# One hybrid attention, SSD and gating layer on one core: first B and C tiles made as a pair, modulation sums in two banks, a store and a norm moved

## Chip, core and metric

One core of a Trainium2 chip runs the whole layer in one launch. The metric is the device time in microseconds (us) of one launch. The kernel before was run three times; the profile is of a fourth execution, whose own time stands beside its span in the table below.

## What is computed

One layer of a diffusion backbone, for 128 context tokens and 512 latent tokens (640 columns together), width 2048. Cut to what matters here:

```python
m = silu(cvec) @ w_mod + b_mod;  shift, scale, gate = split(m, 3)
h = rms(x, g_pre) * (1 + scale) + shift
q, k, v, g_a, xbc, z, dt_raw, u, v_c, g_c, g_m = split(h @ w_in)
o_a = attention(q, k, v) * silu(g_a)
xbc = silu(dwconv(xbc));  x, B, C = split(xbc)      # B and C: 4 tiles of 128 channels each
o_b = rms(ssd(x, dt, B, C) * silu(z))
o_c = u * (w_s @ norm(v_c) + b_s) * silu(g_c)
merged = sigmoid(g_m) gates over o_a @ w_br_a, o_b @ w_br_b, o_c @ w_br_c
y = x + gate * rms(merged @ w_out, g_post)
```

All inputs are float32. The products are made from halves of 32-bit numbers: each operand is split into a high part (type fp32r) and the rest, and three matmuls (high by high, high by rest, rest by high) make one product.

## The kernel before

`h` has its 2048 channels on 16 blocks of 128 partitions, its 640 tokens along the free axis. A tile of 128 output channels is made on TensorE (PE) in one of two ways. `plain` (L208) runs over 16 channel blocks and two halves of 320 tokens: 16 x 2 x 3 = 96 matmuls of 320 columns. `pair` (L219) makes two tiles together by seven block products (in the manner of Strassen and Winograd), each over 8 blocks: 7 x 8 x 3 = 168 matmuls of 320 columns, where two plain tiles take 192. Its weights are combined on GpSimd (POOL, L190 to L198) and split into halves on ScalarE (ACT, `whi`, L166) and VectorE (DVE, `wlo`, L167).

The stages around the change, in the order of the program:

- **First stage** (L340 to L370). For each of 16 channel blocks k: `wm_block` (L262) loads 2 MB of modulation weights in four pieces and sums them on PE into one PSUM bank `m` (sixteen matmuls, L271, which the trace holds as 32 records); DVE copies the bank to `mrow` (L274); two small matmuls with `sel` (L349) turn the row into columns; DVE makes the factors (`mc`, L352, L353) and applies them (`xn`, L357); ACT makes the high half `hh` (L360) and DVE the rest `hl` (L361). Then PE makes the first 512 channels of `v_c` for that block (L331 to L333: ten matmuls with `hh`, five with `hl`, 512 columns each) and the first tile of B (`u`, L368: six matmuls of 320 columns). `h` is also stored to `h_d` in HBM (L359), since `make_t` later reads it back for the operands of the seven products.
- **Rest of v_c** (L381 to L398), then gating norm and mixing, and `dt`.
- **Plain tiles**: the first tile of C (`plain(NT_C, ...)`, with `post_conv` for it and for B's first tile, L635 to L638), then three tiles each of u and g_c; `make_t` and `make_t3` run beside them.
- **Pairs**: five of u and g_c, then the list `rest`: pairs of x, B, C (`xbc`, whose `post_conv` is four DVE operations of 642 columns for each tile), pairs of merge gates (`post_gate`, tanh on ACT), pairs of `silu` tiles, pairs of k, v, q. From the job with number `n0 - 1` on, `Pre` prepares the SSD beside the pairs: 36 steps, one with each of 36 pairs, with its own loads on the queue of SyncE (SP), exponentials on ACT, products on DVE.
- **SSD, attention, branch projections, output**, and at the end, for the last quarter of the output channels, norm, gate and residual (L1296 to L1324).

What sets the order: the scheduler of the framework takes the program's text in order, but places instructions of each engine by its own plan, so that an instruction can stand before others that the text has ahead of it. `issue_after` ties an instruction behind another. Every engine then runs its list in order, and so does SP's list of DMAs.

Of the kernel before, what the change touches and what calls it, by code (L numbers as in the profile page):

```python
# [7 lines left out]
F32 = mybir.dt.float32  # L8
F32R = mybir.dt.float32r
AF = mybir.ActivationFunctionType  # L10
# [24 lines left out]
def hybrid_step(ctx: ExitStack, tc: tile.TileContext, a: dict, o: dict):  # L35
# [106 lines left out]
    wseq = [("plain", NT_C)] + [("plain", n + g) for g in range(NF) for n in (NT_U, NT_GC)]  # L142
    wseq += [("pair", NT_U + g, NT_GC + g) for g in range(NF, 8)]
    gates = [("pair", NT_GM + 16 * b + d, NT_GM + 16 * b + d + 1) for b in (2, 1, 0) for d in range(0, KD, 2)]
    xbc = [(NT_X + t, NT_X + t + 1) for t in range(0, 8, 2)] + [(NT_B + 1, NT_B + 2), (NT_B + 3, NT_C + 1), (NT_C + 2, NT_C + 3)]
# [3 lines left out]
    for x in xbc:  # L149
        rest += [("pair", *x), gates.pop(0)]  # L150
# [127 lines left out]
    bt0 = cvp.tile([P, T], F32, tag="bt0", name="bt0")  # L278
# [44 lines left out]
    u_ps = [ps_tile("u0"), ps_tile("u1")]  # L323
    mps = ps_tile("m")
    vw, uw = {}, {}
# [10 lines left out]
    for k in range(KD + 2):  # L336
        if k < KD:
            mrow[k] = wm_block(wmp, a["w_ms"][k], mps, 9)
            if k % 2 == 0:
                vw[k], vw[k + 1] = load_w(a["w_v0"][:, k:k + 2, :], eng=G)  # L340
            if k % 8 == 0:
                for i, p_ in enumerate(load_w(a["w_nt"][NT_B, :, k:k + 8, :], wmp, "u", 2, eng=G)):
                    uw[k + i] = p_
        if 1 <= k <= KD:

            i = k - 1
            sl_ps = u_ps[0][:, HALF + 4 * i:HALF + 4 * i + 4]
            for s in range(2):
                TE.matmul(sl_ps[:, 2 * s:2 * s + 2], mrow[i][:, s * P:(s + 1) * P], sel, start=(i < 2), stop=True, skip_group_check=True)  # L349
# [12 lines left out]
        if k >= 2:  # L362
            i = k - 2
            v_block(i, range(NCH))
            uh, ul = uw[i]
            for w, x, first, last in ((uh, h_hi, i == 0, False), (uh, h_lo, False, False), (ul, h_hi, False, i == KD - 1)):
                for s in range(2):
                    TE.matmul(u_ps[s][:, :HALF], w, x[i][:, s * HALF:(s + 1) * HALF], start=first, stop=last)  # L368
    st.close()
    with ExitStack() as ph:  # L370
# [4 lines left out]
        for s in range(2):  # L375
            S.copy(bt0[:, s * HALF:(s + 1) * HALF], u_ps[s][:, :HALF])
# [135 lines left out]
    def halves(t):  # L512
        return [t[:, H1], t[:, H2]]

# [267 lines left out]
    n0 = 2 * len(xbc)  # L782
# [485 lines left out]
    for n in range(4):  # L1268
# [32 lines left out]
        for t in range(NCH):  # L1301
# [8 lines left out]
            V.tensor_tensor(ya[t, n], v_ps[t], gb[:, min(t, 1), :], op=ALU.mult)  # L1310
            rs = yp.tile([P, 1], F32, name=f"rs{t}")
            V.reduce_sum(rs, ssy[t], axis=mybir.AxisListType.X)
            rsqrt(rs, rs, 0.0625 / D)
            fin.append(rs)
            for f in {0: (), NCH - 1: (t - 1, t)}.get(t, (t - 1,)):
                dst = o["y_prompt"] if f == 0 else o["y_sample"][(f - 1) * P:f * P]
                for m in range(4):
                    if m == 1 or f < 3 and m == 2:
                        S.activation(ya[f, m], ya[f, m], AF.Copy, scale=fin[f])
                        G.tensor_tensor(xr[f][m], ya[f, m], xr[f][m], op=ALU.add)  # L1320
                    else:
                        V.scalar_tensor_tensor(out=xr[f][m], in0=ya[f, m], scalar=fin[f], in1=xr[f][m],
                                               op0=ALU.mult, op1=ALU.add)
                    nc.sync.dma_start(out=dst[:, m * 512:(m + 1) * 512], in_=xr[f][m])  # L1324
# [89 lines left out]
```

## Time and profile before

| what | value |
|---|---|
| time of a run, median of 3 (lowest to highest) | 2525.13 us (2521.27 to 2529.65) |
| profiled execution, own time | 2523.14 us |
| its span on the core | 2521.3 us |
| PE busy, share of the span | 2430.2 us, 96% |
| DVE, ACT, POOL busy | 1714.3, 1086.2, 805.0 us (68, 43, 32%) |
| mean DMA rate over the span | 163 GB/s |

Busy shares are means over stages with different limits. The rows below go by stage: the view by windows gives the busy time of each engine in a stretch, and the timeline gives single instructions.

### The profile page before, as it was taken

What the parts mean: (1) busy time and instruction counts of PE and PEld (TensorE: products, weight loads), DVE (VectorE), ACT (ScalarE), POOL (GpSimd) and SP (SyncE); (2) the same over time, 40 slices, a digit from 0 to 9 for tenths busy, and PEclk for the clock granted to TensorE, in tenths of its full rate; (3) what the DMA queues carried; (4) which work ended last, traced back from release to release, by engine and by line L of the source; (5) the groups of instructions that cost most, each with busy time, mean ns of one, the idle gap of its engine ahead of it and who ended that gap; (6) DMA issues with size and microseconds to landing.
All of it is one profiled execution on the core that took longest, in us unless ns stands there. A gap on an engine that the chain in (4) does not pass through costs nothing. (4 is left out here: it accounts for less than half of the span.)

```text
span 2521.3 us, 43204 instructions
## 1 busy us (share of the span) xinstructions
PE 2430.2 (96%) x16615; PEld 2298.9 (91%) x16615; DVE 1714.3 (68%) x2769; ACT 1086.2 (43%) x2343; POOL 805.0 (32%) x372
## 2 busy tenths in 40 slices
PE   6989999999999999999999999999999999999998
PEld 4569999999999999999999999989998888998886
DVE  5344688887888778767777677777544555537974
ACT  4122233444444555555555554555323666322222
POOL 2100044444434344434343344334232233331002
PEclk9999999999999999999999999999999999999999
DMA  9943533333333344543444444434987554445545
GB/s 379 351 164 101 164 113 118 105 116 115 105 110 115 130 147 133 161 160 128 150 143 136 137 128 156 143 121 155 333 311 249 174 182 135 155 123 193 177 142 166
DMA packets 154073, 411.13 MB, mean 163 GB/s; under 512 B 16966, under 2 KB 29547, under 8 KB 153867
## 3 DMA queue, kind: packets, MB, share of 16 engines
q1 hardware_dynamic: 151562, 407.33, 48.4%
q8 instruction: 130, 2.13, 0.4%
q10 hardware_dynamic: 2304, 1.05, 0.1%
q14 instruction: 77, 0.62, 0.1%
HBM read 333.50 MB, written 74.81 MB: 162 GB/s over the span
## 5 line engine op out<-in xcount | busy, mean ns | idle before, releaser
L167 DVE TENSOR_TENSOR wlo<-wraw,whi 128x512 fp32r<-128x512 f32 x448 | 607.5, 1373 | 128.7 <-ACT whi L166 120.8
L166 ACT CAST whi<-wraw 128x512 fp32r<-128x512 f32 x448 | 275.1, 616 | 314.9 <-PE acca L235 148.3
L135 ACT CAST whi<-wraw 128x512 fp32r<-128x512 f32 (+1 forms) x238 | 140.1, 592 | 415.6 <-PE bk L820 138.9
L236 PE MATMUL acca<-hh,wlo 128*128 128x320 f32 x896 | 280.5, 313 | 15.3 <-DVE wlo L167 15.3
L166 ACT CAST whi<-s 128x512 fp32r<-128x512 f32 x336 | 203.0, 617 | 207.9 <-PE sm L235 85.1
L167 DVE TENSOR_TENSOR wlo<-s,whi 128x512 fp32r<-128x512 f32 x336 | 232.8, 693 | 73.8 <-ACT whi L166 69.8
L234 PE MATMUL acca<-hh,whi 128*128 128x320 f32 x896 | 278.4, 311 | 0.9 <-ACT whi L166 0.9
L235 PE MATMUL acca<-hl,whi 128*128 128x320 f32 x896 | 277.5, 310 | 0.0
L190 POOL TENSOR_TENSOR s<-wraw 128x1024 f32<-128x1024 f32 x56 | 147.2, 2628 | 368.6 <-DMA wraw<-in_w_nt 226.8
L136 DVE TENSOR_TENSOR wlo<-wraw,whi 128x512 fp32r<-128x512 f32 (+1 forms) x218 | 154.5, 712 | 148.7 <-ACT whi L135 148.1
L191 POOL TENSOR_TENSOR s<-s,wraw 128x1024 f32<-128x1024 f32 x56 | 150.5, 2688 | 258.2 <-DVE wlo L167 258.1
L198 POOL TENSOR_TENSOR s<-wraw,s 128x1024 f32<-128x1024 f32 x56 | 138.6, 2475 | 209.8 <-issue 190.3
L236 PEld LDWEIGHTS acca<-hh,wlo 128*128 128x128 f32 x896 | 168.8, 188 | 21.7 <-DVE wlo L167 21.6
L234 PEld LDWEIGHTS acca<-hh,whi 128*128 128x128 f32 x896 | 169.2, 189 | 1.2 <-ACT whi L166 1.1
L235 PEld LDWEIGHTS acca<-hl,whi 128*128 128x128 f32 x896 | 169.0, 189 | 0.0
L820 PE MATMUL bk<-oh,whi 128*128 128x320 f32 x512 | 164.2, 321 | 0.7 <-DVE c L250 0.7
L820 PE MATMUL bk<-oh,wlo 128*128 128x320 f32 x512 | 158.9, 310 | 0.0
L820 PE MATMUL bk<-ol,whi 128*128 128x320 f32 x512 | 158.8, 310 | 0.0
L236 PE MATMUL sm<-t4h,wlo 128*128 128x320 f32 x448 | 141.6, 316 | 13.3 <-DVE wlo L167 13.3
L192 POOL TENSOR_TENSOR wraw<-wraw 128x1024 f32<-128x1024 f32 x56 | 151.8, 2710 | 4.3
L234 PE MATMUL sm<-t4h,whi 128*128 128x320 f32 x448 | 139.7, 312 | 2.4 <-ACT whi L166 2.4
L235 PE MATMUL sm<-t4l,whi 128*128 128x320 f32 x448 | 139.4, 311 | 0.0
(403 smaller groups left out, 6953.7 us busy)
## 6 DMA issues: line engine op xcount, KB each, us to landing
wraw<-in_w_nt SPq DMA_DIRECT2D x240, 512.0 KB, 3.8
wm<-in_w_ms SPq DMA_DIRECT2D x64, 512.0 KB, 7.1
wraw<-in_w_br SPq DMA_DIRECT2D x48, 512.0 KB, 4.5
wm<-in_w_mg SPq DMA_DIRECT2D x32, 512.0 KB, 3.9
wraw<-in_w_out SPq DMA_DIRECT2D x31, 512.0 KB, 3.9
g_gate<-sg SPq DMA_DIRECT2D x48, 320.0 KB, 2.4
gt<-g_gate SPq DMA_DIRECT2D x48, 320.0 KB, 4.5
ac_d<-Y SPq DMA_DIRECT2D x32, 256.0 KB, 3.4
```

The source lines that it names most:

```text
L135: S.copy(hi[:, :n], rv)
L136: eng.tensor_tensor(lo[:, :n], rv, hi[:, :n].bitcast(F32), op=ALU.subtract)
L166: S.copy(hi, src[:, i:i + 512])
L167: V.tensor_sub(lo, src[:, i:i + 512], hi.bitcast(F32))
L190: G.tensor_tensor(s1, a21, a22, op=ALU.add)
L191: G.tensor_tensor(s2, s1, a11, op=ALU.subtract)
L192: G.tensor_tensor(a21, a11, a21, op=ALU.subtract)
L198: G.tensor_tensor(s2, a12, s2, op=ALU.subtract)
L234: TE.matmul(ps, wh, bh, start=(k == 0 and i not in (2, 3)), stop=False, skip_group_check=True)
L235: TE.matmul(ps, wh, bl, start=False, stop=False, skip_group_check=True)
L236: mm = TE.matmul(ps, wl, bh, start=False, stop=(k == n - 1), skip_group_check=True)
L820: newest[0] = TE.matmul(*args, **kw)
```

## The change

Four edits, in the order of the program:

1. B's first tile is no longer made in the first stage (`u_ps` was two banks, its 96 matmuls and its two weight loads go). One of the two banks becomes a second bank for the modulation sums: `wm_block` alternates between `mps[0]` and `mps[1]`.
2. The store of `h` to `h_d` leaves the first stage's text. In the text of the rest of v_c, for each k, DVE now adds `hh` and `hl` to a tile `hs` and SP stores that.
3. C's first plain tile goes. B and C are now four pairs, so that `xbc` has eight pairs and not seven; the order of `rest` changes with it, and `n0` is 15 and not 14.
4. At the end, each token block's root is started ahead of its product with the gate row, on DVE and POOL; one of ACT's and POOL's pieces of a block goes to DVE; and the outputs of the block before are tied behind both.

```diff
-    wseq = [("plain", NT_C)] + [("plain", n + g) for g in range(NF) for n in (NT_U, NT_GC)]
+    wseq = [("plain", n + g) for g in range(NF) for n in (NT_U, NT_GC)]
...
-    xbc = [(NT_X + t, NT_X + t + 1) for t in range(0, 8, 2)] + [(NT_B + 1, NT_B + 2), (NT_B + 3, NT_C + 1), (NT_C + 2, NT_C + 3)]
+    xbc = [(NT_X + t, NT_X + t + 1) for t in range(0, 8, 2)] + [(NT_B + t, NT_B + t + 1) for t in range(0, 8, 2)]
...
     for x in xbc:
-        rest += [("pair", *x), gates.pop(0)]
+        rest.append(("pair", *x))
+    if x[0] != NT_C + 2:
+        rest.append(gates.pop(0))
...
-    u_ps = [ps_tile("u0"), ps_tile("u1")]
-    mps = ps_tile("m")
+    u_ps = ps_tile("u0")
+    mps = [ps_tile("m"), ps_tile("u1")]
...
-            mrow[k] = wm_block(wmp, a["w_ms"][k], mps, 9)
+            mrow[k] = wm_block(wmp, a["w_ms"][k], mps[k % 2], 9)
...
-            if k % 8 == 0:
-                for i, p_ in enumerate(load_w(a["w_nt"][NT_B, :, k:k + 8, :], wmp, "u", 2, eng=G)):
...
-            nc.sync.dma_start(out=h_dram[:, i, :], in_=hf)
...
-            uh, ul = uw[i]
-            for w, x, first, last in ((uh, h_hi, i == 0, False), (uh, h_lo, False, False), (ul, h_hi, False, i == KD - 1)):
...
+                        if blk == 0:
+                            hs = gp.tile([P, T], F32, tag=("raw", "sg", "c2")[k % 3], name="hs")
+                            V.tensor_tensor(hs, h_hi[k].bitcast(F32), h_lo[k].bitcast(F32), op=ALU.add)
+                            nc.sync.dma_start(out=h_dram[:, k, :], in_=hs)
...
-    post_conv(8, halves(bt0))
-    ac = two_banks()
-    plain(NT_C, ac)
-    post_conv(12, [b[:, :HALF] for b in ac])
...
-    n0 = 2 * len(xbc)
+    n0 = 2 * len(xbc) - 1
...
-            V.tensor_tensor(ya[t, n], v_ps[t], gb[:, min(t, 1), :], op=ALU.mult)
             rs = yp.tile([P, 1], F32, name=f"rs{t}")
             V.reduce_sum(rs, ssy[t], axis=mybir.AxisListType.X)
-            rsqrt(rs, rs, 0.0625 / D)
+            V.tensor_scalar(rs, rs, 0.0625 / D, EPS, op0=ALU.mult, op1=ALU.add)
+            root = G.tensor_tensor(rs, rs, mhalf[:, :1], op=ALU.pow)
+            gated = V.tensor_tensor(ya[t, n], v_ps[t], gb[:, min(t, 1), :], op=ALU.mult)
...
+                with tc.issue_after(gated.ins), tc.issue_after(root.ins):
...
-                    if m == 1 or f < 3 and m == 2:
+                        if m == 1:
```

How instructions stand in the built programs, at three places.

**PE in the first stage**, late in it: from the end of one block's `v_` matmuls to the start of the next block's. L271 and L273 are the modulation sums, L349 and L346 the small matmuls with `sel`. Before:

```order
L333 MATMUL v_466<-whi,hl_1292 128x512
L368 MATMUL u_468<-hl_1292,whi 128x320
L368 MATMUL u_468<-hh_133,wlo 128x320
L271 MATMUL m<-wm,cs 32x256 x12
L349 MATMUL u_467<-sel,mrow 128x2 x2
L271 MATMUL m<-wm,cs 32x256 x4
L368 MATMUL u_467<-hh_133,whi 128x320
L368 MATMUL u_467<-hl_1292,whi 128x320
L368 MATMUL u_467<-hh_133,wlo 128x320
L271 MATMUL m<-wm,cs 32x256 x4
L331 MATMUL v_462<-whi,hh_134 128x512
```

and now:

```order
L334 MATMUL v_465<-whi,hl_1193 128x512
L273 MATMUL u_468<-wm,cs 32x256 x4
L273 MATMUL m<-wm,cs 32x256 x4
L346 MATMUL u_466<-sel,mrow 128x2 x2
L273 MATMUL m<-wm,cs 32x256 x8
L332 MATMUL v_461<-whi,hh_134 128x512
```

The matmuls of B's tile are gone on both sides of the small ones; between the small matmuls and the next block's first there now stand modulation sums alone. The sums go to `m` and `u_468` in turn.

**DVE in the first stage**, one block late in it, from `hl` of one block to `hl` of the next. Before:

```order
L361 TENSOR_TENSOR hl_1166<-xn_115,hh_131 128x640
L274 COPY mrow<-m 128x256
L352 TENSOR_TENSOR mc<-u_467,pc 128x4
L353 TENSOR_SCALAR mc<-mc,pc 128x2
L357 TENSOR_SCALAR xn_116<-xn_116,mc 128x128
L357 TENSOR_SCALAR xn_116<-xn_116,mc 128x512
```

and now:

```order
L357 TENSOR_TENSOR hl_1081<-xn_115,hh_131 128x640
L381 TENSOR_TENSOR hs<-hh_131,hl_1081 128x640
L276 COPY mrow<-u_468 128x256
L349 TENSOR_TENSOR mc<-u_466,pc 128x4
L350 TENSOR_SCALAR mc<-mc,pc 128x2
L354 TENSOR_SCALAR xn_116<-xn_116,mc 128x128
L354 TENSOR_SCALAR xn_116<-xn_116,mc 128x512
```

and SP's list there, in the first stage too (L270 are the loads of modulation weights):

```order
L270 DMA wm<-in_w_ms 128x1024 x3
L125 DMA wraw<-in_w_v 128x544
L382 DMA h_d<-hs 128x640
L270 DMA wm<-in_w_ms 128x1024 x5
L382 DMA h_d<-hs 128x640
```

The new sum `hs` (L381), which the text has in the rest of v_c, is placed by the scheduler in the first stage, right behind `hl` and ahead of the next copy of `mrow`; all sixteen of them stand ahead of DVE's copies that end the stage. Their stores stand among the loads of modulation weights, as the stores of `xn` did.

**SP beside the pairs.** A pair of merge gates ends in two stores to `g_gate`, an x, B or C tile in two to `cv_d`, a `silu` tile in one to `sl_a` or `sl_b`; `ac_d` and `acum_d` belong to `Pre`. Early in `rest`, before:

```order
L529 DMA cv_d<-cv 128x128
L510 DMA cv_d<-cv 128x512
L184 DMA wraw<-in_w_nt 128x1024 x2
L510 DMA g_gate<-sg 128x640 x2
L184 DMA wraw<-in_w_nt 128x1024 x5
L529 DMA cv_d<-cv 128x128
```

and now:

```order
L186 DMA wraw<-in_w_nt 128x1024 x3
L520 DMA cv_d<-cv 128x128
L504 DMA cv_d<-cv 128x512
L186 DMA wraw<-in_w_nt 128x1024
L520 DMA cv_d<-cv 128x128
L504 DMA cv_d<-cv 128x512
```

The eight pairs of x, B and C now follow each other with no gate pair between. Behind them come the eight `silu` pairs, of which seven now have no step of `Pre` (before, all eight had one); the k, v, q pairs have twelve steps as before, and 23 gate pairs have one, where 16 had. A gate pair with its step of `Pre` stands as it did:

```order
L504 DMA g_gate<-sg 128x640 x2
L759 DMA ac_d<-Y 128x512
L672 DMA ssq<-acum_d 128x640
L186 DMA wraw<-in_w_nt 128x1024 x4
L504 DMA g_gate<-sg 128x640 x2
```

## Rows read from the trace of the kernel before

**Rows 1.** The page: busy time (share of the span) and instructions of the engines.

```profile
PE 2430.2 (96%) x16615; PEld 2298.9 (91%) x16615; DVE 1714.3 (68%) x2769; ACT 1086.2 (43%) x2343; POOL 805.0 (32%) x372
```

**Rows 2.** Windows, first stage and pairs: PE, PEld, DVE, ACT, POOL; clock; DMA share, GB/s.

```profile
20.00:80.00 60.00, 50.05 (x386) 31.24 (x383) 28.02 (x84) 15.42 (x38) 16.30 (x14) 0.97 1.03 407
35.00:160.00 125.00, 114.01 (x831) 73.80 (x831) 41.94 (x98) 21.99 (x35) 20.49 (x16) 0.99 0.87 324
398.90:472.90 74.00, 74.00 (x507) 74.00 (x506) 65.33 (x70) 29.27 (x53) 37.52 (x17) 1.00 0.35 113
```

**Rows 3.** One PE block of the first stage (start, length, engine, line).

```profile
63.19 0.50 PE L331 MATMUL v<-whi,hh 128*128 128x512 f32 x1 [0.55 <-ACT hh L360]
...
65.62 0.31 PE L368 MATMUL u<-hh,whi 128*128 128x320 f32 x1
65.87 0.64 PE L271 MATMUL m<-wm,cs 128*32 128x256 f32 x8
...
66.44 1.43 PE L333 MATMUL v<-whi,hl 128*128 128x512 f32 x5
...
67.70 0.31 PE L368 MATMUL u<-hl,whi 128*128 128x320 f32 x1
...
68.66 0.61 PE L349 MATMUL u<-sel,mrow 128*128 128x2 f32 x4
...
71.67 0.50 PE L331 MATMUL v<-whi,hh 128*128 128x512 f32 x1 [0.62 <-ACT hh L360]
```

**Rows 4.** The same chain late in the stage, from `sel` to the next block.

```profile
126.77 0.61 PE L349 MATMUL u<-sel,mrow 128*128 128x2 f32 x4
...
129.49 0.50 PE L331 MATMUL v<-whi,hh 128*128 128x512 f32 x1 [0.34 <-ACT hh L360]
```

**Rows 5.** First matmuls of the first block, and the last block's first.

```profile
35.85 0.80 PE L331 MATMUL v<-whi,hh 128*128 128x512 f32 x1 [1.96 <-ACT hh L360]
...
36.88 0.63 PE L331 MATMUL v<-whi,hh 128*128 128x512 f32 x1
...
160.37 0.50 PE L331 MATMUL v<-whi,hh 128*128 128x512 f32 x1 [1.15 <-ACT hh L360]
```

**Rows 6.** Waits of PE in the first stage (35 to 160 us): total, times, longest.

```profile
PE v L331 <- ACT hh L360: 7.0, 10, 2.0
PE m L271 <- DVE mrow L274: 2.7, 5, 0.5
```

**Rows 7.** POOL's split of weights and DVE's `hl` there: shortest, median, longest (ns).

```profile
L136 POOL TENSOR_TENSOR wlo<-wraw,whi x16: 1267/1276/1355, 37.8 to 134.6; 128x512 fp32r<-128x512 f32 x16
L361 DVE TENSOR_TENSOR hl<-xn,hh x16: 815/825/1421, 35.8 to 160.4; 128x640 fp32r<-128x640 f32 x16
```

**Rows 8.** From the first stage to the rest of v_c.

```profile
164.89 0.49 DVE L613 TENSOR_TENSOR ssq<-tb,ta 128x320 f32<-128x320 f32 x1 [3.71 <-DMA ta<-h_d]
...
167.23 1.88 DVE L374 COPY vc<-v 128x512 f32<-128x512 f32 x3
...
169.25 0.56 PE L391 MATMUL acca<-whi,hh 128*128 128x272 f32 x1 [4.30 <-DVE vc L374]
```

**Rows 9.** Each pair's one copy L240, by stretch: times, first and last start (us).

```profile
L240 ACT COPY u<-acca x15: 403/418/424, 472.9 to 827.2; 128x320 f32<-128x320 f32 x15
L240 ACT COPY u<-acca x9: 416/418/422, 852.3 to 1055.1; 128x320 f32<-128x320 f32 x9
L240 ACT COPY u<-acca x13: 407/418/419, 1055.1 to 1364.9; 128x320 f32<-128x320 f32 x13
L240 ACT COPY u<-acca x16: 402/405/408, 1364.9 to 1765.6; 128x320 f32<-128x320 f32 x16
```

**Rows 10.** Waits of PE beside seven x, B, C and seven gate pairs (473 to 827 us).

```profile
PE acca L236 <- DVE wlo L167: 5.7, 7, 0.8
```

**Rows 11.** The end: DVE's last two entries in the timeline.

```profile
2514.86 1.42 DVE L1322 SCALAR_TENSOR_TENSOR wraw<-y,rs,wraw 128x512 f32<-128x512 f32 x2 [0.66 <-POOL rs L115]
2516.19 0.75 DVE L1322 SCALAR_TENSOR_TENSOR wraw<-bk,rs,wraw 128x512 f32<-128x512 f32 x1
```

More of the change, by code (lines that the diff above doesn't have):

```diff
@@ L277, in hybrid_step @@
     dt_raw = cvp.tile([P, NCH, 32], F32, name="dt_raw")
-    bt0 = cvp.tile([P, T], F32, tag="bt0", name="bt0")
     psx = ExitStack()
@@ L322, in hybrid_step @@
     v_ps = [ps_tile(f"v{t}") for t in range(NCH)]
-    u_ps = [ps_tile("u0"), ps_tile("u1")]
-    mps = ps_tile("m")
-    vw, uw = {}, {}
+    u_ps = ps_tile("u0")
+    mps = [ps_tile("m"), ps_tile("u1")]
+    vw = {}
     def v_block(k, ts):
@@ L337, in hybrid_step @@
         if k < KD:
-            mrow[k] = wm_block(wmp, a["w_ms"][k], mps, 9)
+            mrow[k] = wm_block(wmp, a["w_ms"][k], mps[k % 2], 9)
             if k % 2 == 0:
                 vw[k], vw[k + 1] = load_w(a["w_v0"][:, k:k + 2, :], eng=G)
-            if k % 8 == 0:
-                for i, p_ in enumerate(load_w(a["w_nt"][NT_B, :, k:k + 8, :], wmp, "u", 2, eng=G)):
-                    uw[k + i] = p_
         if 1 <= k <= KD:
             i = k - 1
-            sl_ps = u_ps[0][:, HALF + 4 * i:HALF + 4 * i + 4]
+            sl_ps = u_ps[:, 4 * i:4 * i + 4]
             for s in range(2):
-                TE.matmul(sl_ps[:, 2 * s:2 * s + 2], mrow[i][:, s * P:(s + 1) * P], sel, start=(i < 2), stop=True, skip_group_check=True)
+                TE.matmul(sl_ps[:, 2 * s:2 * s + 2], mrow[i][:, s * P:(s + 1) * P], sel, start=True, stop=True)
             mc = wmp.tile([P, 2, 2], F32, tag="mc", name="mc")
@@ L362, in hybrid_step @@
         if k >= 2:
-            i = k - 2
-            v_block(i, range(NCH))
-            uh, ul = uw[i]
-            for w, x, first, last in ((uh, h_hi, i == 0, False), (uh, h_lo, False, False), (ul, h_hi, False, i == KD - 1)):
-                for s in range(2):
-                    TE.matmul(u_ps[s][:, :HALF], w, x[i][:, s * HALF:(s + 1) * HALF], start=first, stop=last)
+            v_block(k - 2, range(NCH))
     st.close()
@@ L374, in hybrid_step @@
             (S.copy if t % 2 else V.tensor_copy)(vc[:, t, 0:512], v_ps[t])
-        for s in range(2):
-            S.copy(bt0[:, s * HALF:(s + 1) * HALF], u_ps[s][:, :HALF])
         psx.close()
@@ L510, in store @@
         stored[0] = nc.sync.dma_start(out=out, in_=in_)
-    def halves(t):
-        return [t[:, H1], t[:, H2]]
     def post_conv(t, x):
@@ L1309, in hybrid_step @@
                 continue
-            V.tensor_tensor(ya[t, n], v_ps[t], gb[:, min(t, 1), :], op=ALU.mult)
             rs = yp.tile([P, 1], F32, name=f"rs{t}")
             V.reduce_sum(rs, ssy[t], axis=mybir.AxisListType.X)
-            rsqrt(rs, rs, 0.0625 / D)
+            V.tensor_scalar(rs, rs, 0.0625 / D, EPS, op0=ALU.mult, op1=ALU.add)
+            root = G.tensor_tensor(rs, rs, mhalf[:, :1], op=ALU.pow)
             fin.append(rs)
+            gated = V.tensor_tensor(ya[t, n], v_ps[t], gb[:, min(t, 1), :], op=ALU.mult)
             for f in {0: (), NCH - 1: (t - 1, t)}.get(t, (t - 1,)):
                 dst = o["y_prompt"] if f == 0 else o["y_sample"][(f - 1) * P:f * P]
-                for m in range(4):
-                    if m == 1 or f < 3 and m == 2:
[L1319 to L1324, printed above, removed]
+                with tc.issue_after(gated.ins), tc.issue_after(root.ins):
+                    for m in range(4):
+                        if m == 1:
+                            S.activation(ya[f, m], ya[f, m], AF.Copy, scale=fin[f])
+                            G.tensor_tensor(xr[f][m], ya[f, m], xr[f][m], op=ALU.add)
+                        else:
+                            V.scalar_tensor_tensor(out=xr[f][m], in0=ya[f, m], scalar=fin[f], in1=xr[f][m],
+                                                   op0=ALU.mult, op1=ALU.add)
+                        nc.sync.dma_start(out=dst[:, m * 512:(m + 1) * 512], in_=xr[f][m])
 def _layout(i):
```

## The prediction

> **What bounds the kernel now.** I read the page first, then windows by stage, then the timeline inside the stages that the change touches, and last the waits. The page says PE: 2430 us of the span [rows 1]. But that is a mean over stages, and two of them matter here. Between pairs PE is never idle: in three pairs it is busy 74.00 of 74.00 us, and DVE has 65.33 us of work beside it, ACT and POOL much less [rows 2]. So there a matmul costs 74.0/507 = 0.146 us, a pair 74.0/3 = 24.67 us, and what delays DVE may come through to PE. In the first stage PE is busy 114.0 of 125 us [rows 2], and a block is a chain: `sel` on PE, `mc` and `xn` on DVE, `hh` on ACT, back to PE's `v` matmuls. That wait is short, 0.55 to 1.15 us [rows 3 to 5], 7.0 us in ten waits [rows 6], only because matmuls of B's tile and modulation sums lie beside the chain. The DMA rate of 407 GB/s is high early in the stage (20 to 80 us) but falls to 324 over its length at a share of 0.87 [rows 2], and no wait of PE on a load is among the large ones, so I take it that loads set only the stage's start. The sixteen blocks' first matmuls run from 35.85 to 160.37 us [rows 5]: 124.5/15 = 8.30 us a block.
>
> **First stage.** What leaves it: per block six matmuls of B's tile. What does not leave it, whatever the text says: the sum `hs` and the store of `h`; the order has all sixteen in the stage. So part 2 of the change does not move the store in the built program, and adds sixteen DVE operations. None costs PE directly; the question is whether removed PE work was on the chain or filled its gaps. I build a block from the chain. Ten `hh` matmuls take 65.62 − 63.19 = 2.43 us, five `hl` 67.70 − 66.44 = 1.26, a group of four sums (eight records) 66.44 − 65.87 = 0.57 [rows 3]. From `sel` to the next block's first matmul it takes 71.67 − 68.66 = 3.01 us in the block of rows 3 and 129.49 − 126.77 = 2.72 in that of [rows 4]. In both PE had work for most of this and then still waited for `hh`; so it is the chain's own length, and removing the tile's matmuls from within it gives nothing. I take 2.72, since little beside it is left that can delay it.
>
> In the new order `sel` stands behind the five `hl` matmuls in thirteen of fifteen blocks: 13 x (2.43 + 1.26 + 2.72) = 83.3 us. In two it stands ahead of them: 2 x (2.43 + 2.72) = 10.3. The sums that stand ahead of `sel` are on the path: 28 groups of 0.57 us are 16.0, and 1.3 for starting them, from the 0.25 us between neighbours of different kinds (65.62 to 65.87) [rows 3]. Copies of the bank just ahead of `sel` in four blocks cost 2.7/5 = 0.54 us each [rows 6], less what a second bank takes away; I take 0.4, so 1.6. The first block starts at a slower pace, 36.88 − 35.85 = 1.03 us for two matmuls [rows 5] against 0.49; for five of them some 1.3. And DVE is slowed at times beside POOL: `hl` takes 0.815 us at best, 1.421 at worst [rows 7]; three such cases on the chain are 1.8. Sum 83.3 + 10.3 + 17.3 + 1.6 + 1.3 + 1.8 = 115.6, against 124.5: **−8.9**. The two weight loads of B's tile are 1.05 MB, of which half lies ahead of the first block: 0.52 MB at 407 GB/s is **−1.3**. Bounds: if the chain never shows, PE's sum for a block is 2.43 + 1.26 + 4 x 0.57 + some 0.5 = 6.5, so 15 x 1.8 = −27; if the pace stays 8.3 us, −1.3 alone.
>
> At the stage's end DVE now waits 3.71 us for `h_d` in an operation of `make_t`'s chain, and only behind it makes the copies `vc` that free PE, which stood 4.30 us [rows 8]. In the new order the copies stand ahead. The last `hs`, of the length of an `hl` (0.825 [rows 7]), stands ahead of them too, and by then DVE has nothing else to do. PE resumed 169.25 − 160.37 = 8.9 us behind the last block's start [rows 5, 8]; ten and five matmuls (3.7), two copies of 0.63 and their latency make 6.4: **−2.5** (bounds 0 and −3.7). Front in all: −12.7.
>
> DVE's `hs` add costs 0.8 us ahead of the next `mrow`, in a stage where DVE is busy 41.9 of 125 us [rows 2]. A `hl` is ready while PE still has its five matmuls (1.26 us) and often sums before `sel`; I cost it at nothing, covered by those. Without that cover it is 0.8 in each of the four blocks with a late `mrow`, +3; in all of them +12. POOL's splits last 1.27 us [rows 7], and an `hl` beside one was up to 0.6 longer; an `hs` may be so too. The Trainium skill (GPSIMD Engine Reference, section 1, Specifications) has a rule that speaks against this part: GpSimd and VectorE share an SBUF interface and contend when VectorE reads two inputs from SBUF, as `hs` does; by it `hs` could wait for a whole split, +5 in those four blocks, and the sum of all parts would be about +13 in place of +8. The 1.421 us agree with some of that.
>
> **C's plain tile** goes: 96 matmuls x 0.146 = **−14.0**; PE has no idle time there. Its `post_conv`s are DVE work that moves to the new pair.
>
> **The pairs.** One more x, B, C pair comes. In the stretch with seven of these and seven gate pairs without a step of `Pre`, fourteen periods take 827.2 − 472.9 = 354.3 us, 25.31 each [rows 9]. I give the excess over 24.67 (14 x 0.64 = 9.0) to the x, B, C pairs, because PE's waits there are seven (5.7 us), all for `wlo`, DVE's late split [rows 10]: such a pair costs 24.67 + 1.28 = 25.95. Next, the kinds with `Pre`: `silu` pairs 202.8/8 = 25.35, k, v, q 309.8/12 = 25.82, gates 400.7/15 = 26.71 [rows 9]. `Pre` keeps its 36 steps, but now 7 more of them lie on gates, at 26.71 in place of 24.67, and 7 fewer on `silu` pairs, at 24.67 in place of 25.35. So 25.95 + 7 x 2.04 − 7 x 0.68 = 26.0 + 14.3 − 4.8 = **+35.5**. The step on a gate pair is dearer since its two stores, `Pre`'s loads and the next weights share SP's list. Eight x, B, C pairs in a row have no gate pair between them in which DVE catches up. The seven waits come once a pair and do not grow, so I add nothing; the bound is 0 to +8 (twice the wait per pair). The lower bound of the whole is +26: no cost for where `Pre`'s steps lie; the upper +44.
>
> **The end.** DVE waits 0.66 us for POOL's root in the last block [rows 11]. With the root started before the gate product that wait goes, and one more product on DVE comes, of 0.75 [rows 11], in an earlier block with time ahead of the root's result: **−0.5** (−1.5 to +0.5).
>
> **Sum**: −12.7 − 14.0 + 35.5 − 0.5 = **+8.3**. The profiled execution's own time is 2523.1, so 2531.4; the median of the runs is 2.0 above it, so I say **2533.5**. A measurement of this kernel tells about 0.3% (7.6 us) from no change, and the forecast lies just past that: slower is likelier than faster, and "the same" is nearly as likely as slower.
>
> **Rivals.**
> 1. *Not slower: the gate pair's price is of its place, not of its kind.* The fifteen gate periods at 26.71 are the last in the list [rows 9], where `Pre`'s steps are perhaps the larger ones; the first seven gates with a step may go at 25.4 or less. Then 7 x 1.3 = 9.5 goes from the sum: −1, 2524. It decides if early gates with a step run under some 25.5. For it: k, v, q, earlier, cost 0.9 less. Against: a gate pair's two more stores on SP, and tanh beside `Pre`'s exponentials on ACT.
> 2. *The first stage falls to PE's own pace.* With two banks the sums run ahead freely, and `sel` comes early enough that the chain hides; blocks go at 6.9, −21 in place of −8.9: sum −4, 2521. Against: the order has sums alone behind `sel`, under 2.72 us of them.
> 3. *`hs` holds up `mrow`.* It decides where the copy is the last thing before `sel`. One `hs` beside a split costs 0.82 + 0.6 = 1.4 us [rows 7]; in the four blocks 5.7 us come back, sum +14, about 2539. Against: DVE is idle two thirds of the stage.
> 4. *DVE's lag builds up over eight x, B, C pairs in a row*: +8, about 2541. For it: DVE has 65.33 of 74 us in three pairs [rows 2]. Against: the waits are all one kind and short [rows 10].
>
> **How the numbers follow.** Main case 0.46, rivals 0.18, 0.14, 0.12, 0.10. The main case, with a spread of some 7 for the unknown terms, is slower by over 0.3% in 0.26, the same in 0.19, faster in 0.01; rival 1 mostly the same (0.14; 0.03 faster, 0.01 slower), rival 2 the same or faster (0.08; 0.05; 0.01 slower), rival 3 slower (0.10; 0.02 the same), rival 4 slower (0.10). In all 0.09 faster, 0.43 the same, 0.48 slower. The range reaches from rival 2 to beyond rival 4: 2520 to 2546; the main case alone has 2527 to 2540.
>
> **What would show it.** The first-stage blocks at 7.7 us, with PE's wait for `hh` longer than 7.0 in all, right; at 6.9, rival 2; at 8 or more with `mrow` as releaser, rival 3. PE resuming some 6.4 us behind the last block's start. x, B, C pairs at 25.9; at 27, rival 4. The first seven gates with a step at 26.7; at 25.4, rival 1. `silu` without one at 24.7. The forecast is wrong if the front gains under 5 or over 20 us, or the pairs' total differs by less than 26 or more than 44.

## The result, and the profile after

The changed kernel takes 2542.45 us (median of four runs, 2540.53 to 2543.83), the kernel before 2525.27: a ratio of 1.0064, 95% interval 1.0049 to 1.0080. It is slower, by 17 us, where 8.3 were forecast. The profiled execution took 2542.94 us, its span is 2541.2, 19.9 more than that of before [rows 1 has before's busy times]:

```profile
span 2541.2 us, 43203 instructions
PE 2430.2 (96%) x16591; PEld 2304.0 (91%) x16591; DVE 1755.7 (69%) x2803; ACT 1090.1 (43%) x2345; POOL 808.0 (32%) x369
```

PE is busy for the very same 2430.2 us. It has 24 matmul records less, but stands longer and runs longer at the low clock: the granted clock of TensorE is 1.00 over most of both traces and 0.50, the lower of its two levels, in short stretches (from 115.5 to 118.5 us here). Cut at points that both kernels have, the two traces differ so (us; the last column is the prediction's):

| stretch | before | after | difference | forecast |
|---|---|---|---|---|
| to the first block's first matmul | 35.85 | 35.47 | −0.4 | −1.3 |
| from there to the last block's | 124.52 | 118.86 | −5.7 | −8.9 |
| from there to the rest of v_c | 8.88 | 6.09 | −2.8 | −2.5 |
| rest of v_c | 61.65 | 60.39 | −1.3 | 0 |
| from there to the third pair's copy | 168.04 | 162.48 | −5.6 | −14.0 |
| third pair's copy to the last one's | 1366.7 | 1397.6 | +31.0 | +35.5 |
| from there to the branches' first matmul | 18.99 | 19.90 | +0.9 | 0 |
| from there to PE's end | 724.99 | 728.71 | +3.7 | 0 |
| from there to the span's end | 11.73 | 11.68 | −0.1 | −0.5 |

**First stage.** The timeline of PE: the first block's first matmul, a block in the middle, the last block's first, and the first of the rest of v_c (they answer to [rows 5, 8]):

```profile
35.47 0.50 PE L332 MATMUL v<-whi,hh 128*128 128x512 f32 x1 [1.11 <-ACT hh L356]
...
114.84 0.50 PE L332 MATMUL v<-whi,hh 128*128 128x512 f32 x1 [1.62 <-ACT hh L356]
115.18 0.47 PE L333 MATMUL v<-wlo,hh 128*128 128x512 f32 x1
115.45 0.63 PE L332 MATMUL v<-whi,hh 128*128 128x512 f32 x1
115.88 0.63 PE L333 MATMUL v<-wlo,hh 128*128 128x512 f32 x1
...
154.33 0.50 PE L332 MATMUL v<-whi,hh 128*128 128x512 f32 x1 [1.18 <-ACT hh L356]
160.42 0.36 PE L385 MATMUL acca<-whi,hh 128*128 128x272 f32 x1 [2.35 <-DVE vc L365]
```

and PE's waits from 35 to 160 us (total, times, longest; to [rows 6]):

```profile
PE v L332 <- ACT hh L356: 21.2, 15, 2.6
```

The wait for `hh` went from 7.0 us in ten waits to 21.2 in fifteen: what B's tile had filled stands empty now. And behind the gap of 1.62 us the matmuls of one block follow each other at 0.43 us in place of 0.23. Four of the sixteen blocks run at the low clock, one did before, the first. The windows view has the granted clock for 110 to 135 us (busy us of PE, PEld, DVE, ACT, POOL; then the clock):

```profile
110.00:135.00 25.00, 20.53 (x144) 13.34 (x143) 11.08 (x21) 4.03 (x6) 3.81 (x3) 0.88 0.89 314
```

In the same window before it was 1.00, as from 45 to 160 us altogether.

**Ahead of the first pairs.** PE's waits from 305 to 351 us:

```profile
PE sm L238 <- DVE wlo L169: 4.1, 3, 2.8
PE acca L219 <- DVE wlo L136: 2.8, 1, 2.8
```

and the instruction of DVE behind which the split for L219 was queued:

```profile
312.72 0.49 DVE L604 TENSOR_TENSOR t3c<-tb,ta 128x320 f32<-128x320 f32 x1 [3.05 <-DMA tb<-h_d]
```

Before, the same waits (from 325 to 367 us) were these:

```profile
PE acca L217 <- DVE wlo L136: 2.3, 1, 2.3
PE acca L236 <- DVE wlo L167: 1.4, 1, 1.4
```

From v_c's end to the third pair's copy PE stands 9.2 us in all, 3.6 before. It waits for splits of weights, and these stand in DVE's list among the operations of `make_t`, one of which waits for `h_d`. The clock falls twice here (granted 0.83 from 315 to 325 us and from 330 to 340), once before (0.83 from 330 to 340).

**Pairs.** The view by line of each pair's one copy (times, first and last start): before in all, after in all, then after by kind, each kind's list ending with the first copy of the next (x, B, C; `silu` without a step of `Pre`; the first seven gates with one; the other sixteen). These answer to [rows 9]:

```profile
L240 ACT COPY u<-acca x54: 402/418/424, 398.9 to 1765.6; 128x320 f32<-128x320 f32 x54
```

```profile
L242 ACT COPY u<-acca x55: 403/418/422, 383.3 to 1780.9; 128x320 f32<-128x320 f32 x55
L242 ACT COPY u<-acca x9: 420/421/422, 457.2 to 662.1; 128x320 f32<-128x320 f32 x9
L242 ACT COPY u<-acca x8: 419/420/420, 662.1 to 835.7; 128x320 f32<-128x320 f32 x8
L242 ACT COPY u<-acca x8: 405/408/418, 1167.5 to 1349.5; 128x320 f32<-128x320 f32 x8
L242 ACT COPY u<-acca x17: 403/406/409, 1349.5 to 1780.9; 128x320 f32<-128x320 f32 x17
```

An x, B, C pair takes 204.9/8 = 25.61 us, a `silu` pair without a step 24.80, the first seven gates with a step 26.0, the last sixteen 26.96 (15 of them 26.71 before).

**Behind the pairs** the code is the same, yet PE's start is 1.2 us later after the last pair: this wait was 0.68 us before, in front of the same matmul.

```profile
1800.81 0.38 PE L807 MATMUL bk<-oh,whi 128*128 128x320 f32 x1 [1.87 <-DVE c L252]
```

The other 3.7 us come at three places: 1.5 right behind this wait, at a low clock, some 1.0 at SSD's first steps and 1.9 at the last branch, at a low clock too (0.83 from 2185 to 2195 us; 1.00 at the same matmuls before, 2165 to 2175), less 0.7 further on.

**The end.** DVE's last entries, and POOL's:

```profile
2532.32 0.14 DVE L1299 TENSOR_SCALAR rs<-rs 128x1 f32<-128x1 f32 x1
2532.39 0.74 DVE L1312 SCALAR_TENSOR_TENSOR wraw<-sm,rs,wraw 128x512 f32<-128x512 f32 x1
2533.13 3.41 DVE L1312 SCALAR_TENSOR_TENSOR wraw<-y,rs,wraw 128x512 f32<-128x512 f32 x2
2536.47 0.74 DVE L1312 SCALAR_TENSOR_TENSOR wraw<-bk,rs,wraw 128x512 f32<-128x512 f32 x1
```

```profile
2532.55 0.55 POOL L1300 TENSOR_TENSOR rs<-rs,mhalf 128x1 f32<-128x1 f32 x1 [1.72 <-DVE rs L1299]
2533.06 2.93 POOL L1310 TENSOR_TENSOR wraw<-y,wraw 128x512 f32<-128x512 f32 x2
```

DVE no longer waits for the root [rows 11], but now its last products and POOL's fall together: two products take 3.41 us where they took 1.42 [rows 11].

### The profile page after: what moved, and what is told of

Read it like the earlier page. It is cut to its first block, busy times and chain, and to the rows that moved or that the text cites. A ratio compares the mean times of both kernels' runs of the same rounds, so it can differ in the third digit from the quotient of the medians.

```text
span 2541.2 us, 43203 instructions
## 1 busy us (share of the span) xinstructions
PE 2430.2 (96%) x16591; PEld 2304.0 (91%) x16591; DVE 1755.7 (69%) x2803; ACT 1090.1 (43%) x2345; POOL 808.0 (32%) x369
## 5 line engine op out<-in xcount | busy, mean ns | idle before, releaser
L169 DVE TENSOR_TENSOR wlo<-wraw,whi 128x512 fp32r<-128x512 f32 x456 | 622.5, 1382 | 140.0 <-ACT whi L168 134.0
L168 ACT CAST whi<-wraw 128x512 fp32r<-128x512 f32 x456 | 280.6, 617 | 342.7 <-PE acca L237 176.9
L238 PE MATMUL acca<-hh,wlo 128*128 128x320 f32 x912 | 285.9, 313 | 20.6 <-DVE wlo L169 20.6
L169 DVE TENSOR_TENSOR wlo<-s,whi 128x512 fp32r<-128x512 f32 x342 | 239.3, 700 | 71.9 <-ACT whi L168 66.2
L238 PE MATMUL sm<-hh,wlo 128*128 128x320 f32 x456 | 141.9, 311 | 2.9 <-DVE wlo L169 2.8
```

Source lines behind the costliest of these rows:

```text
L168: S.copy(hi, src[:, i:i + 512])
L169: V.tensor_sub(lo, src[:, i:i + 512], hi.bitcast(F32))
L238: mm = TE.matmul(ps, wl, bh, start=False, stop=(k == n - 1), skip_group_check=True)
```

## Experiments

Twelve kernels. "The run" is the median of a kernel's runs; the kernel before, beside them on the same chips, had medians of 2522.0 to 2523.3. The ratio to it has its interval in brackets.

**The gate pairs, put back between the x, B, C pairs.**

```diff
     for x in xbc:
         rest.append(("pair", *x))
-    if x[0] != NT_C + 2:
-        rest.append(gates.pop(0))
+        if x[0] != NT_C + 2:
+            rest.append(gates.pop(0))
```

> The changed kernel, but with seven gate pairs put back between the eight x, B, C pairs; everything else as changed. Theory (where Pre's steps lie costs time): seven gate pairs without a step run at 24.6 us as the silu pairs without one do now, seven more silu pairs get a step (25.25 in place of 24.8), and the seven gate pairs that had a step at 26.0 are gone from the end. From the third pair's copy to the last one's 1390 us in place of 1397.6, the run 2535 us. Rival (order costs nothing, an x, B, C pair and Pre's steps cost the same anywhere): 1397 us there, the run 2542.

Measured: 2544.9 us, 1.0081 [1.0065, 1.0097]. The order alone gave nothing here:

```profile
L242 ACT COPY u<-acca x55: 402/417/421, 385.8 to 1788.6; 128x320 f32<-128x320 f32 x55
```

1402.8 us, not 1390, in the slowest of the six runs (2551.4 us). For this kernel the rival (no gain) holds; with four plain tiles, below, the same order made the run shorter.

**h stored from xn, as before; no sums `hs`.**

```diff
+            nc.sync.dma_start(out=h_dram[:, i, :], in_=hf)
             S.copy(h_hi[i], hf)
...
-                            V.tensor_tensor(hs, h_hi[k].bitcast(F32), h_lo[k].bitcast(F32), op=ALU.add)
-                            nc.sync.dma_start(out=h_dram[:, k, :], in_=hs)
```

> The changed kernel, but h is stored from xn in the first stage as before, and DVE's sixteen sums hs are gone. Theory (hs is on the path where mrow is just in time): the last block of the first stage starts 4 to 6 us earlier, at 149 to 150 us in place of 154.3, and the run is 2537. Rival (hs lies beside PE's work): the last block starts at 154 plus or minus 1, the run 2541 to 2544.

Measured: 2557.1 us, 1.0137 [1.0122, 1.0151]; neither expected it. The last block starts at 158.74 us, 123.2 behind the first, and six blocks run at the low clock (four in the changed kernel). At the stage's end DVE has this order,

```profile
161.58 0.69 DVE L366 COPY vc<-v 128x512 f32<-128x512 f32 x1 [2.04 <-PE v L334]
164.50 0.49 DVE L600 TENSOR_TENSOR ssq<-tb,ta 128x320 f32<-128x320 f32 x1 [2.23 <-DMA ta<-h_d]
164.90 0.68 DVE L366 COPY vc<-v 128x512 f32<-128x512 f32 x1
```

with `make_t`'s first operation, which waits for a load, ahead of the second copy, and PE stands as it did in the kernel before:

```profile
167.52 0.56 PE L381 MATMUL acca<-whi,hh 128*128 128x272 f32 x1 [5.07 <-DVE vc L366]
```

So `hs` was not what held the stage. Its store changed the scheduler's lists, and that the copies stand first is worth 2.7 us at the stage's end. The stage itself is 4.4 us longer than the changed kernel's, most of it by its two more slow blocks (1.6 us each, table below). About 5 us more come in the pairs' stretch (1402.6); see below on how that varies.

**One bank for the sums.**

```diff
-            mrow[k] = wm_block(wmp, a["w_ms"][k], mps[k % 2], 9)
+            mrow[k] = wm_block(wmp, a["w_ms"][k], mps[0], 9)
```

> The changed kernel with one bank for the modulation sums (the second stands unused). Theory (the second bank takes away PE's waits for the copy mrow, 2.7 us in five before, and moves sel earlier in the list): those waits come back, some 0.5 us a block, the last block of the first stage starts 2 to 6 us later (156 to 160 us), the run 2544 to 2549. Rival (the copy was never on the path, PE waits for hh anyway): last block at 151 to 156 as in other executions of this stage, the run 2540 to 2544.

Measured: 2543.7 us, 1.0080 [1.0065, 1.0095]; last block at 151.2, 115.8 us behind the first. The first two rows of PE's waits there:

```profile
PE v L332 <- ACT hh L356: 13.6, 12, 1.6
PE m L273 <- DVE mrow L276: 3.5, 6, 0.8
```

The waits for `mrow` are back, and those for `hh` are shorter in return. The stage has two blocks at the low clock and is as long as the changed kernel's list with two (115.4 to 115.8, table below). The second bank bought nothing.

**Plain tiles for B and C; pairs as before.** From here on "the front kernel".

```diff
-    wseq = [("plain", n + g) for g in range(NF) for n in (NT_U, NT_GC)]
+    wseq = [("plain", NT_B), ("plain", NT_C)] + [("plain", n + g) for g in range(NF) for n in (NT_U, NT_GC)]
...
-    xbc = [(NT_X + t, NT_X + t + 1) for t in range(0, 8, 2)] + [(NT_B + t, NT_B + t + 1) for t in range(0, 8, 2)]
+    xbc = [(NT_X + t, NT_X + t + 1) for t in range(0, 8, 2)] + [(NT_B + 1, NT_B + 2), (NT_B + 3, NT_C + 1), (NT_C + 2, NT_C + 3)]
...
+    for t, n in ((8, NT_B), (12, NT_C)):
+        ac = two_banks()
+        plain(n, ac)
+        post_conv(t, [b[:, :HALF] for b in ac])
```

(with gates between and `n0` as before)

> The changed kernel's first stage and end, but the pairs as before: B's and C's first tiles are both made by plain products after the first stage, seven x, B, C pairs alternate with gate pairs. Theory (the front gives back 10 us up to the end of v_c, and the plain tiles hide make_t): 10.1 us earlier at the end of v_c, plus 14.0 for B's plain tile, minus up to 3.6 of waits ahead of the first pair: 0 to +4 against before, 2525 to 2529, with PE waiting under 1 us ahead of the first pair. Rival (the front's gain is lost again further on, as plain C's was): over 2532.

Measured: 2515.0 us, 0.9972 [0.9961, 0.9982]: faster than both kernels. The first stage has the changed kernel's list of PE, but one block at the low clock in place of four; the last block starts at 148.71. The block with the gap of 1.62 us above is here

```profile
112.30 0.50 PE L330 MATMUL v<-whi,hh 128*128 128x512 f32 x1 [1.63 <-ACT hh L354]
112.64 0.39 PE L331 MATMUL v<-wlo,hh 128*128 128x512 f32 x1
112.87 0.39 PE L330 MATMUL v<-whi,hh 128*128 128x512 f32 x1
```

with the same gap, and the clock did not fall. From v_c's end to the third pair's copy it takes 178.1 us with PE standing 1.4: with eight plain tiles ahead of the pairs `make_t` is hidden.

**Four plain tiles each of u and g_c**, in the changed kernel.

```diff
-NF = 3
+NF = 4
```

> The changed kernel, but four tiles each of u and g_c are plain and not three, so that there is one pair less: 24 matmuls more in all (3.5 us), and 28 us more PE work between v_c and the first pair. Theory (the first pair waits since make_t's chain on DVE is late, and the plain tile of C had covered it): PE's waits of 9.2 us around the first pair fall to 2 or less, and a fall of the clock there goes with them; 3.5 minus 7 to 9 gives 2537 to 2539. Rival (the pair's own weights are late, whatever lies ahead): the waits stay, the run is 2546.

Measured: 2529.0 us, 1.0018 [1.0010, 1.0027], 12 us under the changed kernel by the ratios, for 3.5 us more of matmuls. PE stands 1.4 us ahead of the pairs, not 9.2. The theory holds, and the price of the missing cover was larger than it said. From v_c's end to the last pair's copy the kernel needs 10.2 us less in spite of the 3.5 of matmuls (162.5 + 1397.6 against 178.1 + 1371.8): 13.7 less of waits and low clock. Another 4.0 are saved behind the pairs; these were not expected.

**The same, with the gates between.** The edit is that of the first run.

> The kernel with four plain tiles each of u and g_c (2529), and the gate pairs put between the x, B, C pairs; 56 pairs as before the change. Theory (the place of Pre's steps costs 7 us, which the kernel with 57 pairs and the gates between hid by a longer time behind): from the third pair's copy to the last one's 1363 to 1367 in place of 1371.8, the run 2520 to 2524. Rival (the order of the pairs costs nothing): 1369 to 1374, the run 2527 to 2531.

Measured: 2520.0 us, 0.9991 [0.9981, 1.0002], 7 us under the kernel without it by the ratios (9 by the medians, from two chips). The copies of the two, first with the pairs of x, B, C in a row, then with gates between:

```profile
L242 ACT COPY u<-acca x54: 402/417/422, 399.6 to 1771.4; 128x320 f32<-128x320 f32 x54
```

```profile
L242 ACT COPY u<-acca x54: 401/417/422, 395.1 to 1760.8; 128x320 f32<-128x320 f32 x54
```

1371.8 and 1365.7, as the theory had it. But PE is busy 1337.4 and 1332.2 us of these, so that it stands only 0.9 us longer in the first; and in the first the clock falls at three places (granted 0.66 from 1360 to 1365, 1517 to 1522 and 1729 to 1734 us), in the second at none. At 0.66 over 5 us each gives up some 1.7 us, together 5.1 of the 6.1. Over all runs of the two kernels the mean granted clock is the same, 0.993. So this order is faster by some 7 us, but that the place of `Pre`'s steps in the pairs' stretch is what gives them is not shown.

**B's tile stays; edit 2 alone, and `make_t` tied behind the copies**, in the kernel before.

```diff
-            nc.sync.dma_start(out=h_dram[:, i, :], in_=hf)
...
-            (S.copy if t % 2 else V.tensor_copy)(vc[:, t, 0:512], v_ps[t])
+            cp = (S.copy if t % 2 else V.tensor_copy)(vc[:, t, 0:512], v_ps[t])
...
+                        if blk == 0:
+                            hs = gp.tile([P, T], F32, tag=("raw", "sg", "c2")[k % 3], name="hs")
+                            V.tensor_tensor(hs, h_hi[k].bitcast(F32), h_lo[k].bitcast(F32), op=ALU.add)
+                            nc.sync.dma_start(out=h_dram[:, k, :], in_=hs)
...
-            make_t(k)
+            with tc.issue_after(cp.ins):
+                make_t(k)
```

> The kernel before with edit 2 alone (h_d stored from hs, text in the rest of v_c), and make_t's first operation tied behind the copies vc. B's tile stays in the first stage, one bank for the sums. Theory (h's new store helps the stage by itself, and the copies' place gives 2.7 us at the stage's end and 1.3 in the rest of v_c, where the clock no longer falls): PE resumes 6.1 us behind the last block's start, the last block starts at 157 to 160, the run is 2517 to 2521. Rival (the gain of the stage is all B's tile): last block at 160 to 162, the run 2521 to 2525.

Measured: 2516.5 us, 0.9976 [0.9962, 0.9991]. Last block at 160.3, where it was: the store does nothing for the stage. The copies' place gives the first part of the gain:

```profile
167.29 0.36 PE L395 MATMUL acca<-whi,hh 128*128 128x272 f32 x1 [2.35 <-DVE vc L373]
```

1.9 us less behind the last block. Another 1.3 in the rest of v_c (60.4) and 1.9 up to the third pair's copy came with it; the 1.3 are the clock's, see below.

**Eight matmuls more behind `sel`**, in the changed kernel and, second, in the front kernel. Their result is thrown away.

```diff
-                TE.matmul(sl_ps[:, 2 * s:2 * s + 2], mrow[i][:, s * P:(s + 1) * P], sel, start=True, stop=True)
+                at_sel = TE.matmul(sl_ps[:, 2 * s:2 * s + 2], mrow[i][:, s * P:(s + 1) * P], sel, start=True, stop=True)
+            if i >= 2:
+                with tc.issue_after(at_sel.ins):
+                    for j in range(8):
+                        TE.matmul(u_ps[:, 128:448], h_hi[0][:, 0:P], h_hi[0][:, 0:320], start=True, stop=True)
```

> The changed kernel with eight matmuls more behind sel in each block of the first stage from the third on (320 columns, 0.15 us each, their result is thrown away, y is unchanged). Theory (without B's tile PE stands 1.1 to 2.6 us in most blocks, and behind some of these gaps the granted clock falls: four blocks have ten hh matmuls of 3.4 to 3.6 us and not 2.2): at most two such blocks are left, and the last block starts at 149 to 152 us in place of 154.3, the run 2538 to 2541. Rival (gaps and clock have nothing to do with each other; the stage is the chain from sel to hh): three to five slow blocks, the last block at 154 or later, since 14 x 1.2 us of matmuls are partly in the way.

Measured: 2540.1 us, 1.0062 [1.0038, 1.0086]; last block at 156.2, the stage 121.0 us (118.9 in the changed kernel).

> The kernel with plain tiles of B and C (changed first stage, pairs as before) and the same eight matmuls in each block (result thrown away). It had one slow block of sixteen in its profile without them. Theory: nothing is left to gain in a good execution; the last block starts at 148.7 plus or minus 1, the run is 2514 to 2516, and the bad executions (2519 to 2521) become rarer. Rival (the added matmuls cost what they last): the last block at 152 or later, the run 2518 to 2522.

Measured: 2533.0 us, 1.0032 [1.0021, 1.0044]; last block at 155.1. In the front kernel PE's wait for `hh` all but goes (20.9 us without the matmuls):

```profile
PE v L330 <- ACT hh L358: 4.4, 3, 2.6
```

and the stage is 7 us longer: 120.9 in place of 114.0. In each, the clock falls once in the stage (granted 0.83 from 40 to 50 us, 1.00 from 50 to 155), so one block is slow; three others also take 2.9 us or more for their ten `hh` matmuls, but these are cut by sums, at full clock. In this the first theory was right, one slow block in place of four, and yet filling the gaps did not pay: the added matmuls stood in the way of the chain. That gaps are what lowers the clock fits this and is not shown, since the lists changed too and the front kernel had one slow block without the matmuls. The second kernel's profile is 17 us longer than the front kernel's, and 7.8 of these lie in the pairs (1369.9 us, 1362.1 there), where nothing was edited and PE stands 36.6 us in place of 28.7; why is open.

**The turn of the banks `sm` set back behind the pairs.**

```diff
+    turn[0] = 0
     branch = {}
```

> The changed kernel, with the turn of the four PSUM banks sm set back to the first one behind the last pair (57 pairs of three banks leave it at the fourth, 56 leave it at the first). Theory (the 4 us that the stages behind the pairs became longer come from this turn): from the last pair to the first matmul of the branches 1.0 to 1.3 us in place of 2.2, and from there to PE's end 725 in place of 729; the run 2538. Rival (it comes from the pairs' count in another way or from the clock at random): 2.2 and 728 to 730 stay, the run 2542.

Measured: 2547.5 us, 1.0087 [1.0064, 1.0110]. From the start of the last pair's last matmul to that of the branches' first it takes 1.6 us (2.2 in the changed kernel, but 1.6 in four others with 57 pairs too), and from there to PE's end 729.2: the turn is not the cause.

**Two plain tiles each of u and g_c**, in the front kernel: six plain tiles and 57 pairs, as in the changed kernel.

```diff
-NF = 3
+NF = 2
```

> The kernel with plain tiles of B and C (2515), with two plain tiles each of u and g_c: six plain tiles ahead of the first pair as in the changed kernel, 57 pairs as there, x, B, C and gates as before. 24 matmuls less than 2515 had: 3.5 us. Theory (the cover of make_t, and 57 pairs): PE waits 6 to 9 us around the first pair, the third copy comes 162 to 165 us behind v_c's end, so 12 us of the 28 that two plain tiles take are lost; the stages behind the pairs are 3 to 5 us longer; the run 2523 to 2529. Rival (the losses come from the pairs of B and C): no wait, 150 us, the run 2511 to 2513.

Measured: 2535.3 us, 1.0050 [1.0035, 1.0065]: 20 us over the front kernel, with 3.5 us of matmuls less. PE's waits between v_c's end and the third pair's copy:

```profile
PE sm L236 <- DVE wlo L167: 3.9, 2, 3.7
PE acca L236 <- DVE wlo L167: 2.1, 2, 1.6
```

The third copy comes 156.8 us behind v_c's end; without waits it would be 178.1 − 28.0 (192 matmuls of 0.146) = 150.1. So 6.7 us are lost by cover, less than expected. The last sixteen gate periods are 27.0 us each (26.5 in the front kernel), and the branches to PE's end 728.1 (725.3): the losses in the pairs and behind them come without B's and C's pair too.

**One of post_conv's four operations on ACT**, in the front kernel.

```diff
-        V.tensor_scalar(y, xq[:, 1:643], cw[:, 1:2], cwh[:, t:t + 1], op0=ALU.mult, op1=ALU.add)
+        S.activation(y, xq[:, 1:643], AF.Identity, scale=cw[:, 1:2], bias=cwh[:, t:t + 1])
```

> The kernel with plain tiles of B and C (2515), with the first of post_conv's four DVE operations (one tap and the bias, 642 columns) made on ACT. Theory (an x, B, C pair costs 1.1 to 1.3 us more than a u and g_c pair since post_conv's operations stand ahead of a split on DVE that PE waits for): with 0.6 us less of them for each tile PE's waits for wlo shrink, the fourteen periods with seven such pairs take 345 to 350 us in place of 354.4, the run 2507 to 2512. Rival (the split waits for a stretched operation beside POOL, or ACT's copies become late in turn): 354 or more, the run 2514 to 2519.

Measured: 2514.8 us, 0.9969 [0.9958, 0.9980], the same as the front kernel. PE's waits beside the seven pairs:

```profile
PE sm L236 <- DVE wlo L167: 4.0, 6, 0.7
PE acca L236 <- DVE wlo L167: 0.7, 1, 0.7
```

5.7 us became 4.7 and moved on by one product. Fourteen periods take 353.4 us, not 354.4. The theory is wrong in the size: most of the price is not these 0.6 us on DVE.

## Why the prediction was right in its direction and too small

**First stage: the mechanism right, the clock mis-sized.** The forecast was a chain of 115.6 us with one slow block in it. Eight kernels have the changed kernel's list on PE for this stage. Sorted by how many of their sixteen blocks ran at the low clock (ten `hh` matmuls over 2.5 us from first to last start):

| slow blocks | stage, first block's start to last block's (us) |
|---|---|
| 1 | 114.0 |
| 2 | 115.4, 115.7, 115.8 |
| 3 | 117.4 |
| 4 | 118.8, 118.9, 119.3 |

Each slow block costs some 1.6 us, and without any the chain would be about 112.4. The mean of the eight is 116.9: the step "13 x (2.43 + 1.26 + 2.72)" and the groups of sums held. With one slow block, as forecast, the stage took 114.0, so that sum was 1.6 too long. What failed is the term of 1.3 us for a slower pace, put on the first block alone; the profiled execution had four such blocks. That the clock might fall where PE stands 21.2 us in place of 7.0 was not in the forecast; the runs with added matmuls, with one slow block each, speak for that cause without showing it.

Rival 2 is out: no execution came near 6.9 us a block (103 us). Rival 3 as well: the sums `hs` last 0.82 us, one of sixteen 1.8, and without them the stage was not shorter.

```profile
L381 DVE TENSOR_TENSOR hs<-hh,hl x16: 816/824/1795, 36.5 to 155.2; 128x640 f32<-128x640 f32 x16
```

The Trainium skill's rule (GPSIMD Engine Reference, section 1, Specifications) that an operation with two inputs in SBUF contends with GpSimd shows in that one sum, about 1 us, not the 5 that the forecast weighed.

**Stage's end:** −2.5 forecast, −2.8 measured, and the mechanism shown by the run with h from xn. The 1.3 us in the rest of v_c were not forecast, and are no gain of the change: the clock at its start was 0.85 before and 1.00 after over ten microseconds, and where it was 0.83 or 0.85 in kernels with the same short gap this stretch took 61.8 to 62.5 us again.

**Plain C is the step that failed.** The forecast said "PE has no idle time there" and took 96 x 0.146 = 14.0 us. The 14 us were cover for `make_t`, whose chain of loads and DVE operations runs beside the plain tiles and holds the splits of weights behind it. Without waits the stretch would have been 150.1 us (above); it was 162.5, so 12.4 are lost. Before, with seven plain tiles, 168.0 against 164.1: 3.9 lost. The difference, 8.5 us, is what the term was wrong by; 5.6 of it is PE standing (9.2 against 3.6), another 1.7 the second stretch of low clock. Eight plain tiles in either kernel bring the standing to 1.4 us. The front kernel with six lost 6.7 and not 12.4, so the price hangs on what else stands there, too.

**The pairs' term was about right, two of its parts not.** +31.0 against +35.5; other kernels with 57 pairs, over the same stretch, are between 1393 and 1404 us, so this sum has some 5 us of spread. An x, B, C pair cost 25.61 us (25.95 forecast) and did not grow over eight in a row: rival 4 is out. The first seven gates with a step took 26.0 us, between forecast (26.7) and rival 1 (25.4). Rival 1's point, under 25.5, was not reached (and its 7 x 1.3 is 9.1, not 9.5). The forecast's two terms for where `Pre`'s steps lie made 9.5 us. No run shows them: the order alone gave nothing with 57 pairs, some 7 us by the medians' ratios with 56, and there the pairs' stretch differs mostly by the clock.

**Behind the pairs** 4.6 us came that no step had. All seven kernels with 57 pairs take 727.9 to 729.6 us from the branches' first matmul to PE's end; six of the seven with 56 pairs take 723.4 to 725.7, the seventh, with the added matmuls, 727.0. The bank turn is not it. In the changed kernel's profile most of the 3.7 us lies at the two stretches of low clock that before does not have (1.5 and 1.9 us); but others of the seven (727.9 and 729.2) have no more such stretches than before, so the clock alone is not it either. What the one pair more changes there is open. That the last sixteen gates are dearer in most of these kernels (26.9 to 27.2, with one exception of 26.4) is open too.

**The end** gave 0.1 us, not 0.5: the wait went, and contention took its place.

So 8.3 became 19.9 in the profiled pair of executions: +8.4 from plain C, +4.6 behind the pairs, +2.6 in the front (more slow blocks, less the 1.3), +0.4 at the end, less 4.5 in the pairs. Between medians it is 17.2. This split is that of one execution each: the profiled one has the lowest mean clock of the four, 0.989, and two with 0.993 took 2540.5 and 2543.8 us, so the same time can be lost in other places. The range held the result; the likeliest case's own range (to 2540) did not. That it was held is in part luck: its upper end was set beyond rival 4, which did not come, and the time came near it by terms that the sum did not have.

## What to carry to other kernels

Before a piece of work is taken off the bounding engine at full price, look at what runs beside it on the others: PE had no idle time during plain C, and still 8.5 of its 14 us were cover for a chain that came due right behind. The front kernel takes B's tile out of the first stage but spends it, as a plain tile, just where that chain needs cover, and has the pairs as before; 24 matmuls more, and by the ratios 23 us less than the changed kernel. An order that a scheduler makes is part of an edit: the part of the new store's gain that could be traced, 2.7 us, came from three copies that moved ahead of a waiting operation.

## What the runs showed of the hardware that was not expected

The granted clock is not given by the list of instructions. Eight programs with the same list in the stage had one to four slow blocks, and the same gap of 1.62 us was followed by spacings of 0.43 us in one and of 0.23 in another. The forecast of such a stage needs a spread of some 5 us for that alone.

DVE beside POOL can be slowed far more than the 0.6 us of [rows 7]. In the kernel before, DVE's operations with two inputs of 320 columns, 0.48 us alone, took as long as POOL's sum beside them. First DVE, then POOL:

```profile
325.98 2.69 DVE L594 TENSOR_TENSOR t4l<-tb,t4h 128x320 fp32r<-128x320 f32 x1
328.60 2.67 DVE L616 TENSOR_TENSOR u<-c,u 128x320 f32<-128x320 f32 x1
331.19 0.48 DVE L594 TENSOR_TENSOR t12l<-c,t12h 128x320 fp32r<-128x320 f32 x1
```

```profile
325.58 2.74 POOL L191 TENSOR_TENSOR s<-s,wraw 128x1024 f32<-128x1024 f32 x1
328.29 2.63 POOL L192 TENSOR_TENSOR wraw<-wraw 128x1024 f32<-128x1024 f32 x1
```

Here one operation of DVE goes for each of POOL's. In these traces the price of a collision goes by what is left of POOL's instruction when DVE's begins, and not by a share of DVE's own: the `hs` of 1.8 us above began at 99.18 us, beside a split of POOL that ran from 98.94 to 100.29, and lasted until 0.7 us behind it. An operation that began ahead of POOL's was not lengthened: 0.48 us for the one at 322.76 us in the kernel before, where POOL's next began at 322.81.
